# Gate and up projections of a feed-forward layer: two of eight weight chunks as seven block products, and a reciprocal cut in four

## The chip, the cores and the metric

The kernel runs on one core of a Trainium2 chip. The metric is the device time of one execution in microseconds, given as the median of several runs. The core has a matrix engine (TensorE, PE in the profile; its weight loads are listed apart as PEld), a vector engine (VectorE, DVE), a scalar engine (ScalarE, ACT), GpSimd (POOL) and a sync engine (SyncE, SP) that issues most of the transfers. Each engine works through its own instructions in the order in which they stand in its program.

## The reference, cut to what matters

One layer of a streaming encoder on 256 tokens of 2048 features, in float32. The first two thirds of the layer are four token mixers behind one wide projection; the last third is a feed-forward layer. What the change touches is the feed-forward layer and one expression of the gated linear attention:

```python
def gla_mixer(zg, w_a2, b_a, head_gain):            # gated linear attention
    ...
    log_a = jax.nn.log_sigmoid(w_lr @ w_a2 + b_a) / GLA_LOGIT_NORM
    ...
def reference(x, ...):
        ...
        h = rms_norm(x, norm_ffn_pre[l])
        ffn = (jax.nn.silu(h @ w_gate[l]) * (h @ w_up[l])) @ w_down[l]
        x = x + rms_norm(ffn, norm_ffn_post[l])
```

`w_gate` and `w_up` are 2048 x 5632, `w_down` is 5632 x 2048.

## The kernel before

Every large product is made of three: each float32 operand is split into a part `hi` that the matrix engine takes as it is and a rest `lo`, and hi·hi, hi·lo and lo·hi are added up in PSUM (lo·lo is left out).

Weights arrive in chunks of 256 rows by 512 columns (512 KB, `Stream.chunk`, L590 to L602): SP issues the transfer into one of four buffers `raw`; ACT casts `raw` to `hi` (L600); DVE subtracts to get `lo` (L601). Three pairs hi, lo exist at a time. A scheduler orders the instructions of each engine by its own cost model; the chunks' cast and subtraction have a raised priority, so that they run one or two chunks ahead of the products.

`gemm_tok` (L661 to L663) multiplies with the activations as the stationary operand (128 rows by 128 tokens) and the weights as the moving one (512 columns). A chunk has two row blocks of 128 and the tokens two halves of 128, so a chunk is 2 x 2 x 3 = 12 products of 512 columns. `gemm_feat` (L692, L693, L695) has it the other way round, the weights stationary and 256 tokens moving; it is used in the first third of the kernel.

The feed-forward part runs over 11 column groups `g` of 512 columns. For each, `gemm_tok` does 8 chunks of `w_gate` into two PSUM banks (one per token half) and 8 chunks of `w_up` into two others. When a gate column is done, ACT takes the sigmoid (L1044) and DVE forms the silu (L1045); when the up column is done, DVE multiplies (L1048), PE transposes the result block by block into a bank `tq` (L1053; eight small products per group) and ACT copies it to the buffer `aT` (L1054). After the eleven groups the down projection starts: ACT casts `aT` to `ah` (L1063), DVE makes `al` (L1064), and PE multiplies with the chunks of `w_down` (L1075 to L1077). All eight PSUM banks are in use: four `mm`, four `tq`, which the down projection's `wd` replaces.

In the gated linear attention, well ahead of this, one reciprocal over 128 x 512 numbers stands on DVE (L421) between the chunk work of a projection that runs at the same time.

## Time and profile before

| | us |
|---|---|
| median of 3 runs | 1647.31 (1645.69 to 1647.57) |
| the profiled execution | 1645.97 |
| its span, first to last instruction | 1644.2 |
| PE busy | 1630.3 (99%) |
| PEld busy | 1384.2 (84%) |
| DVE busy | 994.8 (61%) |
| ACT busy | 759.6 (46%) |
| POOL busy | 33.1 (2%) |
| granted clock of PE, mean | 0.998 of full |

Busy time of PE is counted from the start of a product to its modelled end, and products overlap; how fast products follow one another is therefore read from the difference of their starts in the timeline, not from the duration beside them. A weight load is a separate instruction that stands ahead of each product.

### The profile page before, as it was taken

How to read it: one execution, taken by the hardware profiler on the slowest of the kernel's cores; microseconds unless marked ns; L12 is line 12 of the kernel's file. 1: busy time of each engine (PE TensorE's matmuls, PEld its weight loads, DVE VectorE, ACT ScalarE, POOL GpSimd, SP SyncE). 2: the span in 40 equal slices, each digit the busy share in tenths (PEclk: the TensorE clock that was granted, in tenths of full speed). 3: DMA queues.
4: the chain of work that ended last, by engine and by line, in shares of the span. 5: the costliest groups of instructions: out<-in, count | busy, mean ns of one | idle time of the engine just before them, and what ended most of it. 6: DMA issues, size and time to landing. Idle time of an engine off the chain costs nothing.

```text
span 1644.2 us, 21813 instructions
## 1 busy us (share of the span) xinstructions
PE 1630.3 (99%) x8632; PEld 1384.2 (84%) x8632; DVE 994.8 (61%) x1176; ACT 759.6 (46%) x879; POOL 33.1 (2%) x46
## 2 busy tenths in 40 slices
PE   9999999999999999999999999999999999999997
PEld 9999988887789978888888888888888888888886
DVE  7568784669764477455655655444544555556555
ACT  6353443346554355444444644444444444445443
POOL 0000110000000001000000000000000000000000
PEclk9999999999999999999999999999999999999999
DMA  8554565345556545765555565555555555555563
GB/s 297 181 168 149 180 213 178 130 143 165 171 164 196 187 158 184 269 192 184 190 192 196 191 191 190 186 189 191 191 187 189 188 193 191 190 194 191 193 194 139
DMA packets 86118, 306.84 MB, mean 187 GB/s; under 512 B 9600, under 2 KB 12176, under 8 KB 85504
## 3 DMA queue, kind: packets, MB, share of 16 engines
q1 hardware_dynamic: 84352, 298.85, 55.6%
q0 software_dynamic: 1232, 5.95, 1.2%
q8 instruction: 67, 1.10, 0.3%
q10 hardware_dynamic: 432, 0.66, 0.2%
q14 instruction: 35, 0.29, 0.1%
HBM read 302.40 MB, written 3.01 MB: 186 GB/s over the span
## 4 chain that ended last, share of the span: by engine, by line
PE 97%; issue 1%; ACT 1%; DVE 1%; DMA 0%; POOL 0%; DVEq 0%; POOLq 0%; ACTq 0%
PE mm L662 22%; PE mm L663 21%; PE mm L661 21%; PE mm L692 5%; PE mm L693 4%; PE mm L695 4%; PE mm L1075 2%; PE mm L1077 2%; PE mm L1076 2%; PE wd L1077 2%; PE wd L1076 2%; PE wd L1075 2%; PE tq L1053 1%; PE mm L679 0%; PE ps L465 0%
## 5 line engine op out<-in xcount | busy, mean ns | idle before, releaser
L601 DVE TENSOR_TENSOR lo<-raw,hi 128x1024 fp32r<-128x1024 f32 (+1 forms) x554 | 676.6, 1222 | 550.9 <-ACT hi L600 548.7
L600 ACT CAST hi<-raw 128x1024 fp32r<-128x1024 f32 (+1 forms) x554 | 582.4, 1051 | 721.4 <-PE mm L663 510.1
L662 PE MATMUL mm<-lo,h_hi 128*128 128x512 f32 x704 | 274.9, 390 | 0.0
L663 PE MATMUL mm<-hi,h_lo 128*128 128x512 f32 x704 | 273.9, 390 | 0.1
L661 PE MATMUL mm<-hi,h_hi 128*128 128x512 f32 x704 | 250.6, 391 | 0.2 <-ACT h_hi L361 0.2
L662 PE MATMUL mm<-lo,hT_hi 128*128 128x512 f32 x608 | 238.8, 393 | 2.3 <-DVE lo L601 2.3
L663 PE MATMUL mm<-hi,hT_lo 128*128 128x512 f32 x608 | 237.5, 391 | 0.0
L661 PE MATMUL mm<-hi,hT_hi 128*128 128x512 f32 x608 | 219.5, 391 | 0.0
L692 PE MATMUL mm<-hT_hi,hi 128*128 128x256 f32 (+2 forms) x640 | 178.8, 284 | 0.3 <-ACT hi L600 0.3
L693 PE MATMUL mm<-hT_lo,hi 128*128 128x256 f32 (+2 forms) x640 | 177.1, 281 | 0.3 <-DVE hT_lo L362 0.3
L695 PE MATMUL mm<-hT_hi,lo 128*128 128x256 f32 x576 | 161.6, 282 | 0.0
L661 PEld LDWEIGHTS mm<-hi,h_hi 128*128 128x128 f32 x704 | 132.2, 188 | 27.8 <-ACT h_hi L361 0.9
L663 PEld LDWEIGHTS mm<-hi,h_lo 128*128 128x128 f32 x704 | 132.2, 188 | 27.6 <-DVE s L643 0.5
L662 PEld LDWEIGHTS mm<-lo,h_hi 128*128 128x128 f32 x704 | 132.2, 188 | 27.0
L662 PEld LDWEIGHTS mm<-lo,hT_hi 128*128 128x128 f32 x608 | 114.2, 188 | 27.2 <-DVE lo L601 2.7
L661 PEld LDWEIGHTS mm<-hi,hT_hi 128*128 128x128 f32 x608 | 114.1, 188 | 24.1
L663 PEld LDWEIGHTS mm<-hi,hT_lo 128*128 128x128 f32 x608 | 114.2, 188 | 23.6 <-issue 0.3
L692 PEld LDWEIGHTS mm<-hT_hi,hi 128*128 128x128 f32 (+2 forms) x640 | 119.8, 187 | 2.1 <-ACT hi L600 0.8
L693 PEld LDWEIGHTS mm<-hT_lo,hi 128*128 128x128 f32 (+2 forms) x640 | 120.1, 188 | 1.4 <-DVE hT_lo L362 0.5
L695 PEld LDWEIGHTS mm<-hT_hi,lo 128*128 128x128 f32 x576 | 108.7, 189 | 0.6
L1077 PE MATMUL mm<-hi,al 128*128 128x512 f32 x168 | 65.4, 389 | 0.0
L1076 PE MATMUL mm<-lo,ah 128*128 128x512 f32 x168 | 65.4, 389 | 0.0
(367 smaller groups left out, 1688.3 us busy)
## 6 DMA issues: line engine op xcount, KB each, us to landing
raw<-in_w_in_dram SPq DMA_DIRECT2D x224, 512.0 KB, 3.5
raw<-in_w_gate_dram SPq DMA_DIRECT2D x88, 512.0 KB, 3.5
raw<-in_w_up_dram SPq DMA_DIRECT2D x88, 512.0 KB, 3.5
raw<-in_w_down_dram SPq DMA_DIRECT2D x88, 512.0 KB, 3.5
raw<-in_w_branch_dram SPq DMA_DIRECT2D x32, 512.0 KB, 4.0
raw<-in_w_out_dram SPq DMA_DIRECT2D x32, 512.0 KB, 3.5
raw<-in_w_l_dram SPq DMA_DIRECT2D x8, 464.0 KB, 7.3
xs<-in_x_dram POOLq DMA_DIRECT2D x1, 2048.0 KB, 12.2
```

The costliest lines, as they stand in the source:

```text
L600: nc.scalar.copy(hi[:, :, :w], raw[:, :, :w])
L601: nc.vector.tensor_tensor(lo[:, :, :w], raw[:, :, :w], hi[:, :, :w].bitcast(F32), op=ALU.subtract)
L661: mm(banks[i_], ah[:, ts], hi[:, k, :], start=kt == 0, stop=False)
L662: mm(banks[i_], ah[:, ts], lo[:, k, :], start=False, stop=False)
L663: mm(banks[i_], al[:, ts], hi[:, k, :], start=False, stop=kt == nk - 1)
L692: mm(ps, hi[:, k, cs], hT_hi[:, kt, :], start=first, stop=False, skip_group_check=True)
L693: mm(ps, hi[:, k, cs], hT_lo[:, kt, :], start=False, stop=False, skip_group_check=True)
L695: mm(ps, lo[:, k, cs], hT_hi[:, kt, :], start=False, stop=last, skip_group_check=True)
L1053: T.transpose(ps[:, k, i * 128:(i + 1) * 128], sg[:, i, (2 * kp + k) * 128:(2 * kp + k + 1) * 128], ident)
L1075: mm(bk[j][i], ah[:, k, ts], hi[:, k, :], start=kt == 0, stop=False)
L1076: mm(bk[j][i], ah[:, k, ts], lo[:, k, :], start=False, stop=False)
L1077: mm(bk[j][i], al[:, k, ts], hi[:, k, :], start=False, stop=kt == 43)
```

## The change

In the groups g = 1 to 10, chunks 2 and 5 of each gate column and each up column (40 chunks in all) are no longer 12 products of 512 columns. The chunk is taken as a 2 x 2 matrix of blocks (128 rows by 256 columns each) and the tokens' part as 2 x 2 blocks of 128, and the product of the two is formed by the Winograd form of Strassen's scheme: 7 block products instead of 8, each of them three products (hi and lo) of 256 columns, so 21 products of 256 columns. Three of the seven use raw weight blocks and come first in the new buffers; four use sums of blocks. For that:

- DVE builds the sums of weight blocks in a buffer `t` (L1205 to L1207: 512, 256 and 256 columns), ACT casts seven blocks instead of four (in two pieces, 768 and 1024 columns), and DVE subtracts seven (L1212).
- The sums of activation blocks are built once, in group 0, on POOL (ten operations), ACT and DVE (`Seven.sums`).
- Partial results that belong to more than one output gather in two further banks `px` and `py`, which take the place of two of the four `tq` banks; at the end of each column `close` (L1234 to L1241) adds them up: ACT copies one block, DVE does three additions, and two more with the banks `mm`. The results lie in a buffer `w7`, and the sigmoid, the silu and the multiplication read them there.
- The down projection's buffers (`ah`, `al`, `fg`, `sqf`, the second gain) come from a pool `F2` that is opened after the pool `U` of the new buffers is closed, in the same memory. The transfer of the second gain moves behind the eleven groups.
- The reciprocal becomes four of 128 x 128.

Three places of the engines' programs show what moves. PE where the last up column ends and the down projection begins; before (L663 is the last up column, L1075 to L1077 the down projection, L1053 the transposes of the last group):

```order
L1075 MATMUL mm<-hi,ah 128x512 x2
L1076 MATMUL mm<-lo,ah 128x512
L1077 MATMUL mm<-hi,al 128x512
L1075 MATMUL mm<-hi,ah 128x512
L1076 MATMUL mm<-lo,ah 128x512
L1077 MATMUL mm<-hi,al 128x512
L1076 MATMUL mm<-lo,ah 128x512
L1077 MATMUL mm<-hi,al 128x512
L1075 MATMUL mm<-hi,ah 128x512
L1076 MATMUL mm<-lo,ah 128x512
L1077 MATMUL mm<-hi,al 128x512
L1053 MATMUL tq<-ident,sg 128x128 x8
```

and now (L663 to L665 the up column, L1084 the transposes, L1109 to L1111 the down projection):

```order
L665 MATMUL mm<-hi,h_lo 128x512
L663 MATMUL mm<-hi,h_hi 128x512
L664 MATMUL mm<-lo,h_hi 128x512
L665 MATMUL mm<-hi,h_lo 128x512
L1084 MATMUL tq<-ident,sg 128x128 x8
L1109 MATMUL mm<-hi,ah 128x512
L1110 MATMUL mm<-lo,ah 128x512
L1109 MATMUL mm<-hi,ah 128x512
L1110 MATMUL mm<-lo,ah 128x512
L1111 MATMUL mm<-hi,al 128x512
```

The transposes stood behind eleven entries of the down projection; now they stand ahead of its first product.

DVE around one column's end, before (L601 is a chunk's `lo`, L1045 the silu of a gate column, L1048 the multiplication after an up column):

```order
L1045 SCALAR_TENSOR_TENSOR sg<-mm,r_8015,sg 128x512
L601 TENSOR_TENSOR lo<-raw,hi 128x1024 x7
L1048 TENSOR_TENSOR sg<-sg,mm 128x512 x2
L601 TENSOR_TENSOR lo<-raw,hi 128x1024 x8
L1045 SCALAR_TENSOR_TENSOR sg<-mm,r_8015,sg 128x512
L601 TENSOR_TENSOR lo<-raw,hi 128x1024
L1045 SCALAR_TENSOR_TENSOR sg<-mm,r_8015,sg 128x512
L601 TENSOR_TENSOR lo<-raw,hi 128x1024 x7
L1048 TENSOR_TENSOR sg<-sg,mm 128x512 x2
```

and now, one column's end (L1205 to L1207 and L1212 the sums and rests of a chunk in seven blocks, L1235 to L1241 the closing sums, L1072 the silu; the number behind a name is a buffer's):

```order
L1235 TENSOR_TENSOR w_12059<-w_12059,px 128x256
L1236 TENSOR_TENSOR w_12059<-w_12059,py 128x256
L1237 TENSOR_TENSOR w_12059<-py,w_12059 128x2x256
L1205 TENSOR_TENSOR t<-raw 128x512
L604 TENSOR_TENSOR lo<-raw,hi 128x1024
L1206 TENSOR_TENSOR t<-t,raw 128x256
L1212 TENSOR_TENSOR lo_12184<-raw,hi_12183 128x768
L1241 TENSOR_TENSOR w_12059<-w_12059,mm 128x512 x2
L1207 TENSOR_TENSOR t<-t,raw 128x256
L604 TENSOR_TENSOR lo<-raw,hi 128x1024
L1072 SCALAR_TENSOR_TENSOR sg<-w_12059,r_8018,sg 128x512 x2
L604 TENSOR_TENSOR lo<-raw,hi 128x1024
```

Between two runs of `lo` there were two instructions; now the pieces of two seven-block chunks and the closing sums are mixed in.

DVE around the reciprocal, before (L421 is the reciprocal, L601 the `lo` of chunks, L422 to L426 what the attention does with the reciprocal):

```order
L421 RECIPROCAL h<-h 128x512
L601 TENSOR_TENSOR lo<-raw,hi 128x1024 x3
L422 TENSOR_TENSOR x<-x,h 128x512
L423 TENSOR_TENSOR s_3899<-x 128x512
L601 TENSOR_TENSOR lo<-raw,hi 128x1024
L424 TENSOR_SCALAR h<-s_3899 128x512
L426 SCALAR_TENSOR_TENSOR h<-h,s_3899 128x512 x2
```

and now (the same steps are L424 to L429, `lo` is L604):

```order
L424 RECIPROCAL h<-h 128x128 x4
L604 TENSOR_TENSOR lo<-raw,hi 128x1024 x3
L425 TENSOR_TENSOR x<-x,h 128x512
L426 TENSOR_TENSOR s_3899<-x 128x512
L427 TENSOR_SCALAR h<-s_3899 128x512
L429 SCALAR_TENSOR_TENSOR h<-h,s_3899 128x512
L604 TENSOR_TENSOR lo<-raw,hi 128x1024
```

The four pieces stand one behind the other, and the same three `lo` behind all of them; the next `lo` has moved behind two more steps of the attention.

The diff:

```diff
--- before.py
+++ after.py
@@ -418,7 +418,10 @@
     S.activation(x, x, AF.Exp, scale=-1.0)
 
     V.tensor_scalar(h, x, 2.0, None, op0=ALU.add)
-    V.reciprocal(h, h)
+    for j in range(2):
+        for p in range(2):
+
+            V.reciprocal(h[:, j, p * 128:(p + 1) * 128], h[:, j, p * 128:(p + 1) * 128])
     V.tensor_tensor(x, x, h, op=ALU.mult)
     V.tensor_tensor(s2, x, x, op=ALU.mult)
     V.tensor_scalar(h, s2, 1.0 / 17, None, op0=ALU.mult)
@@ -620,6 +623,7 @@
         e.dram = ctx.enter_context(tc.tile_pool(name="dr", bufs=1, space=bass.MemoryType.DRAM))
         mmp = ctx.enter_context(tc.tile_pool(name="mmp", bufs=1, space=PSUM))
         stream = Stream(e, ring)
+        e.ring = ring
 
         def bank():
             return mmp.tile([128, 512], F32, tag="mm", name="mm", bufs=4)
@@ -642,6 +646,25 @@
 
             V.tensor_scalar(ssum, ssum, 1.0 / n, eps, op0=ALU.mult, op1=ALU.add)
             G.tensor_tensor(ssum, ssum, e.mhalf.to_broadcast(list(ssum.shape)), op=ALU.pow)
+
+        def gemm_seven(w, lhs, banks, seven):
+
+            px, py = seven.banks()
+            for kc in range(8):
+                if kc in seven.kcs:
+                    seven.products(kc, lhs, seven.chunk(w(kc)), banks, px, py, kc == seven.kcs[0])
+                    continue
+                hi, lo = stream.chunk(w(kc))
+                for k in range(2):
+                    kt = 2 * kc + k
+                    ah, al = lhs(kt)
+                    for i in range(2):
+                        ts = slice(i * 128, (i + 1) * 128)
+                        mm(banks[i], ah[:, ts], hi[:, k, :], start=kt == 0, stop=False, skip_group_check=True)
+                        mm(banks[i], ah[:, ts], lo[:, k, :], start=False, stop=False, skip_group_check=True)
+                        mm(banks[i], al[:, ts], hi[:, k, :], start=False, stop=kt == 15, skip_group_check=True)
+            with tc.high_priority(offset=e.boost):
+                return seven.close(banks, px, py)
 
         def gemm_tok(w, lhs, nk, banks, runs={}, into={}):
 
@@ -1032,26 +1055,37 @@
         with ExitStack() as fctx:
             F = fctx.enter_context(tc.tile_pool(name="F", bufs=1))
             aT = F.tile([128, 44, 256], F32, name="aT")
-            gain = F.tile([128, 2048], F32, name="gain2")
-            nc.gpsimd.dma_start(gain, post_ffn.unsqueeze(0).to_broadcast([128, 2048]))
-            with tc.tile_pool(name="tq", bufs=1, space=PSUM) as tq:
+            lhs2 = lambda kt: (h2_hi[:, kt], h2_lo[:, kt])
+            with tc.tile_pool(name="U", bufs=1) as U, tc.tile_pool(name="tq", bufs=1, space=PSUM) as tq:
+                seven = Seven(e, U, tq, (2, 5))
                 for g in range(11):
                     bg, bu = [bank(), bank()], [bank(), bank()]
-                    lhs2 = lambda kt: (h2_hi[:, kt], h2_lo[:, kt])
                     sg = F.tile([128, 2, 512], F32, tag="sg", name="sg", bufs=2)
-                    gemm_tok(columns(w_gate, g), lhs2, 16, bg, {0: 3} if g == 0 else {})
+                    if g == 0:
+                        gemm_tok(columns(w_gate, g), lhs2, 16, bg, {0: 3})
+                        zg = bg
+                        seven.sums(h2_hi, h2_lo)
+                    else:
+                        zg = gemm_seven(columns(w_gate, g), lhs2, bg, seven)
                     for i in range(2):
-                        S.activation(sg[:, i], bg[i], AF.Sigmoid, scale=r2[:, i, 0:1])
-                        V.scalar_tensor_tensor(sg[:, i], bg[i], r2[:, i, 1:2], sg[:, i], op0=ALU.mult, op1=ALU.mult)
-                    gemm_tok(columns(w_up, g), lhs2, 16, bu)
+                        S.activation(sg[:, i], zg[i], AF.Sigmoid, scale=r2[:, i, 0:1])
+                        V.scalar_tensor_tensor(sg[:, i], zg[i], r2[:, i, 1:2], sg[:, i], op0=ALU.mult, op1=ALU.mult)
+                    if g == 0:
+                        gemm_tok(columns(w_up, g), lhs2, 16, bu)
+                        zu = bu
+                    else:
+                        zu = gemm_seven(columns(w_up, g), lhs2, bu, seven)
                     for i in range(2):
-                        V.tensor_tensor(sg[:, i], sg[:, i], bu[i], op=ALU.mult)
+                        V.tensor_tensor(sg[:, i], sg[:, i], zu[i], op=ALU.mult)
                     for kp in range(2):
-                        ps = tq.tile([128, 2, 256], F32, tag="tq", name="tq", bufs=4)
+                        ps = tq.tile([128, 2, 256], F32, tag="tq", name="tq", bufs=2)
                         for k in range(2):
                             for i in range(2):
                                 T.transpose(ps[:, k, i * 128:(i + 1) * 128], sg[:, i, (2 * kp + k) * 128:(2 * kp + k + 1) * 128], ident)
                         S.copy(aT[:, 4 * g + 2 * kp:4 * g + 2 * kp + 2], ps)
+            F = fctx.enter_context(tc.tile_pool(name="F2", bufs=1))
+            gain = F.tile([128, 2048], F32, name="gain2")
+            nc.gpsimd.dma_start(gain, post_ffn.unsqueeze(0).to_broadcast([128, 2048]))
             wd = fctx.enter_context(tc.tile_pool(name="wd", bufs=1, space=PSUM))
             fg = F.tile([128, 2, 2048], F32, name="fg")
             sq = F.tile([128, 512], F32, name="sqf", bufs=2)
@@ -1127,6 +1161,88 @@
                     (nc.sync, nc.scalar)[g % 2 * i].dma_start(outr[:, i, cs], fg[:, i, cs])
 
 
+class Seven:
+    def __init__(self, e, pool, psum, kcs):
+        self.e, self.pool, self.psum, self.kcs = e, pool, psum, kcs
+        n = len(kcs)
+        pad = lambda name, w: pool.tile([128, w], F32R, name=name)
+        self.s_hi, self.s_lo = (pad(n_, 4 * 128 * n).rearrange("p (c b t) -> p c b t", c=n, b=4) for n_ in ("s_hi", "s_lo"))
+
+    def sums(self, h_hi, h_lo):
+
+        e, nc = self.e, self.e.nc
+        G = nc.gpsimd
+        for c, kc in enumerate(self.kcs):
+            t = self.pool.tile([128, 4, 256], F32, tag="t", name="t", bufs=2)
+            h, s = t[:, 0:2], t[:, 2:4].rearrange("p x (b t) -> p (x b) t", t=128)
+            G.tensor_tensor(h, h_hi[:, 2 * kc:2 * kc + 2].bitcast(F32), h_lo[:, 2 * kc:2 * kc + 2].bitcast(F32), op=ALU.add)
+            a11, a21, a12, a22 = h[:, 0, 0:128], h[:, 0, 128:256], h[:, 1, 0:128], h[:, 1, 128:256]
+            G.tensor_tensor(s[:, 0], a21, a22, op=ALU.subtract)
+            G.tensor_tensor(s[:, 2], a11, a21, op=ALU.subtract)
+            G.tensor_tensor(s[:, 1], s[:, 0], a11, op=ALU.subtract)
+            G.tensor_tensor(s[:, 3], a12, s[:, 1], op=ALU.add)
+            nc.scalar.copy(self.s_hi[:, c], s)
+            nc.vector.tensor_tensor(self.s_lo[:, c], s, self.s_hi[:, c].bitcast(F32), op=ALU.subtract)
+
+    def banks(self):
+
+        return [self.psum.tile([128, 2, 256], F32, tag=n, name=n, bufs=1) for n in ("px", "py")]
+
+    def chunk(self, ap):
+
+        e, nc = self.e, self.e.nc
+        G = nc.vector
+        with e.tc.high_priority(offset=e.boost):
+            raw = e.ring.tile([128, 2, 512], F32, tag="raw", name="raw", bufs=e.nraw)
+            nc.sync.dma_start(raw, ap)
+            b = raw.rearrange("p k (c n) -> p (k c) n", c=2)
+            t = self.pool.tile([128, 4, 256], F32, tag="t", name="t", bufs=2)
+            G.tensor_tensor(t[:, 0:2], b[:, 1:3], b[:, 0:1].to_broadcast([128, 2, 256]), op=ALU.add)
+            G.tensor_tensor(t[:, 2], t[:, 0], b[:, 2], op=ALU.add)
+            G.tensor_tensor(t[:, 3], t[:, 2], b[:, 3], op=ALU.add)
+            hi, lo = (self.pool.tile([128, 1920], F32R, tag=n, name=n, bufs=2)[:, 48:1840].rearrange("p (b n) -> p b n", n=256)
+                      for n in ("hi7", "lo7"))
+            for x, o in ((b[:, 1:4], slice(0, 3)), (t, slice(3, 7))):
+                nc.scalar.copy(hi[:, o], x)
+                nc.vector.tensor_tensor(lo[:, o], x, hi[:, o].bitcast(F32), op=ALU.subtract)
+        return hi, lo
+
+    def products(self, kc, lhs, ch, banks, px, py, first):
+
+        mm = self.e.nc.tensor.matmul
+        hi, lo = ch
+        c = self.kcs.index(kc)
+        a = lambda k, i: tuple(x[:, i * 128:(i + 1) * 128] for x in lhs(2 * kc + k))
+        s = lambda b: (self.s_hi[:, c, b], self.s_lo[:, c, b])
+        for (ah, al), b, ps, st in ((a(0, 0), 0, px[:, 0], first), (a(1, 0), 2, banks[0][:, 256:512], False),
+                                    (s(3), 1, banks[0][:, 0:256], False), (s(0), 3, py[:, 1], first), (s(2), 4, py[:, 0], False),
+                                    (s(1), 5, px[:, 1], False), (a(1, 1), 6, banks[1][:, 256:512], False)):
+            mm(ps, ah, hi[:, b], start=st, stop=False, skip_group_check=True)
+            mm(ps, ah, lo[:, b], start=False, stop=False, skip_group_check=True)
+            mm(ps, al, hi[:, b], start=False, stop=kc == self.kcs[-1], skip_group_check=True)
+
+    def close(self, banks, px, py):
+
+        nc = self.e.nc
+        V = nc.vector
+        w = self.pool.tile([128, 5, 256], F32, tag="w7", name="w7", bufs=1)
+        nc.scalar.copy(w[:, 2], px[:, 0])
+        V.tensor_tensor(w[:, 0], w[:, 2], px[:, 1], op=ALU.add)
+        V.tensor_tensor(w[:, 4], w[:, 0], py[:, 0], op=ALU.add)
+        V.tensor_tensor(w[:, 1:4:2], py[:, 1:2].to_broadcast([128, 2, 256]), w[:, 0:5:4], op=ALU.subtract)
+        out = []
+        for i in range(2):
+            o = w[:, 1 + 2 * i:3 + 2 * i].rearrange("p b n -> p (b n)")
+            V.tensor_tensor(o, o, banks[i], op=ALU.add)
+            out.append(o)
+        return out
+
+
 class TagPool:
 
 
```

## Rows read from the trace of the kernel before

**Rows 1.** The page: engines' busy time, chain of waits, one DMA issue (landing us last).
```profile
PE 1630.3 (99%) x8632; PEld 1384.2 (84%) x8632; DVE 994.8 (61%) x1176; ACT 759.6 (46%) x879; POOL 33.1 (2%) x46
...
PE 97%; issue 1%; ACT 1%; DVE 1%; DMA 0%; POOL 0%; DVEq 0%; POOLq 0%; ACTq 0%
...
raw<-in_w_gate_dram SPq DMA_DIRECT2D x88, 512.0 KB, 3.5
```

**Rows 2.** The longest wait of PE: engine line waited for: us, times, longest.
```profile
PE mm L662 <- DVE lo L601: 2.3, 1, 2.3
```

**Rows 3.** Timeline of PE (start, us, instruction), gate and up products, 512 columns.
```profile
1001.01 0.40 PE L662 MATMUL mm<-lo,h_hi 128*128 128x512 f32 x1
...
1011.23 0.39 PE L662 MATMUL mm<-lo,h_hi 128*128 128x512 f32 x1
```

**Rows 4.** Timeline of PE where 256-column products stand, three places.
```profile
308.51 0.39 PE L663 MATMUL mm<-hi,oT 128*128 128x512 f32 x1
308.74 0.28 PE L692 MATMUL mm<-hT_hi,hi 128*128 128x256 f32 x1
...
309.56 0.28 PE L693 MATMUL mm<-hT_lo,hi 128*128 128x256 f32 x1
...
329.45 0.28 PE L692 MATMUL mm<-hT_hi,hi 128*128 128x256 f32 x1
...
332.85 0.28 PE L692 MATMUL mm<-hT_hi,hi 128*128 128x256 f32 x1
...
515.70 0.28 PE L692 MATMUL mm<-hT_hi,hi 128*128 128x256 f32 x1
...
516.88 0.28 PE L693 MATMUL mm<-hT_lo,hi 128*128 128x256 f32 x1
```

**Rows 5.** Busy time by window: PE, PEld, DVE, ACT, POOL, clock, DMA share, GB/s.
```profile
540.00:560.00 20.00, 20.00 (x173) 20.00 (x172) 8.79 (x8) 7.34 (x7) 0.00 (x0) 1.00 0.56 190
1000.00:1100.00 100.00, 100.00 (x453) 82.97 (x452) 49.65 (x45) 43.92 (x47) 0.00 (x0) 1.00 0.57 188
```

**Rows 6.** Groups of instructions by line: count, busy us, mean ns, idle before.
```profile
L601 DVE TENSOR_TENSOR lo<-raw,hi 128x1024 fp32r<-128x1024 f32 x546 | 667.7, 1223 | 549.7 <-ACT hi L600 547.5 <-issue 1.8
L600 ACT CAST hi<-raw 128x1024 fp32r<-128x1024 f32 x546 | 574.8, 1053 | 717.2 <-PE mm L663 510.1 <-PE mm L693 128.7 <-PE mm L1077 53.5
...
L1063 ACT CAST ah<-aT 128x512 fp32r<-128x512 f32 x44 | 27.5, 624 | 56.0 <-PE wd L1076 56.0
...
L1045 DVE SCALAR_TENSOR_TENSOR sg<-mm,r,sg 128x512 f32<-128x512 f32 x22 | 16.4, 747 | 5.4 <-ACT sg L1044 5.4
...
L1048 DVE TENSOR_TENSOR sg<-sg,mm 128x512 f32<-128x512 f32 x22 | 14.0, 679 | 0.0
...
L362 DVE SCALAR_TENSOR_TENSOR hT_lo<-acc,vec,hT_hi 128x256 fp32r<-128x256 f32 x16 | 6.7, 479 | 0.0
...
L458 ACT ACT_TABLE_LOAD x2 | 2.6, 1283 | 0.0
```

**Rows 7.** The sigmoid line L1044: durations, first and last start.
```profile
L1044 ACT ACTIVATE sg<-mm,r x22: 677/688/690, 928.3 to 1373.8; 128x512 f32<-128x512 f32 x22
```

**Rows 8.** Timeline around the end of the last up product, PE, then DVE.
```profile
1394.15 0.39 PE L663 MATMUL mm<-hi,h_lo 128*128 128x512 f32 x1
1394.37 0.61 PE L1075 MATMUL mm<-hi,ah 128*128 128x512 f32 x2
...
1397.10 1.04 PE L1053 MATMUL tq<-ident,sg 128*128 128x128 f32 x8
...
1394.08 1.28 DVE L1048 TENSOR_TENSOR sg<-sg,mm 128x512 f32<-128x512 f32 x2
```

**Rows 9.** Timeline around the reciprocal, DVE, then the PE row that waits.
```profile
372.17 3.34 DVE L421 RECIPROCAL h<-h 128x512 f32<-128x512 f32 x1
375.43 3.42 DVE L601 TENSOR_TENSOR lo<-raw,hi 128x1024 fp32r<-128x1024 f32 x3
...
376.64 0.50 PE L662 MATMUL mm<-lo,hT_hi 128*128 128x512 f32 x1 [2.29 <-DVE lo L601]
```

## The prediction

> **What bounds the kernel now.** I read the page first: PE is busy 99% of the span and the chain that ended last runs through PE for 97% [rows 1]. Next the waits of PE: the longest is one of 2.3 us for a `lo`, and nothing else is worth a microsecond once the kernel has started [rows 2]. So time is won only by fewer or quicker products, and is lost wherever another engine lets PE stand. Then the timeline of PE inside the gate and up columns: 45 products lie between 1001.01 and 1011.23, so one of 512 columns takes 0.2271 us [rows 3], and a chunk of 12 takes 2.725 us. A column group lasts (1373.8 - 928.3) / 10 = 44.55 us by the sigmoid's first and last start [rows 7]. In this stretch DVE is busy 49.65 of 100 us and ACT 43.92, PE's weight loads 82.97 [rows 5]. DVE and ACT have room, half of it at most.
>
> **The products of the seven-block chunks.** 40 chunks change from 12 x 512 columns to 21 x 256. What one of 256 costs is read where such products run now, and the trace shows two levels. From 308.74 to 309.56 seven steps, 0.117 us each; from 515.70 to 516.88 ten steps, 0.118; from 329.45 to 332.85 thirty steps, 0.1133 [rows 4]. The lower level is half of a 512-column step. At the upper level the weight loads are busy all of the time, 20.00 of 20 us [rows 5], so there the loads and not the moving columns seem to set the pace. The first two places are those where 256-column products follow directly on 512-column ones (308.51 is the last of these before the first place), and that is how a seven-block chunk stands between its neighbours; so I take 0.118. A chunk then takes 21 x 0.118 = 2.478 us, 0.247 less than 2.725, and 40 of them save **9.9 us**. At 0.1133 a chunk takes 2.379, and 40 save 13.8 us. The change would gain nothing at a step of 2.725 / 21 = 0.1298, which no row comes near.
>
> A rule of the Trainium skill speaks to this (page "TensorE: Matmul & The Clock Gate", section "Back-to-back issue gap"): an isolated product follows the last after N / 2.4 + 2.5 ns on a full clock, and in a stream of loads and products both set the distance. By its formula 256 columns take 109.2 ns and 512 take 215.8, which would save 2.590 - 2.293 = 0.297 us a chunk, 11.9 us in all. The rows stand above both figures, and the measurement decides; the second half of the rule agrees with the loads at 100%.
>
> **The work for DVE and ACT.** DVE's prices: 1.223 us for 1024 columns (L601) and 0.679 for 512 (L1048) [rows 6], that is 1.06 ns a column and 0.136 us fixed, by which 256 columns take 0.41 and 768 take 0.95 (the nearest row of 256, L362, has 0.479). A seven-block chunk costs DVE 0.68 + 0.41 + 0.41 for the sums and 0.95 + 1.22 for the rests, 3.67 us instead of 1.22. The closing sums of a column cost 0.41 + 0.41 + 3 x 0.68 = 2.86. A column group then has 12 x 1.223 + 4 x 3.67 + 2 x 2.86 + 2 x 0.747 + 2 x 0.68 = 37.9 us of DVE work in 44.55 - 4 x 0.247 = 43.56 us: 87% where there was half. ACT has per chunk 0.84 + 1.05 instead of 1.05 (between L1063's 0.624 for 512 columns and L600's 1.053 for 1024), and a small copy per column: about 24 us a group. Since both prepare chunks ahead, I walked one column through DVE's order: at a column's end the closing sums wait for PE's last product, and behind them stand a `t`, a `lo` and the pieces of the next column's first seven-block chunk. The `lo` of the second chunk of a column still comes about 3.4 us before PE needs it, the silu's products about 2.6 us before the transposes. DVE also waits for transfers in order now, since the sums read `raw` and not ACT's cast; a transfer lands 3.5 us after its issue [rows 1], and I find about 1 us of such waiting per column, within the 43.56 - 37.9 = 5.7 us that a group has free. I cost all of it at **nothing**; if the cover is gone it costs what rival C says. The sums of the activations run once, beside 16 chunks of group 0 that do not need them, and delay the first sigmoid by at most 2 us, when its PSUM bank is not asked for until 22 us later: nothing. The later transfer of the second gain is needed half a down projection later: nothing.
>
> **The border to the down projection.** Before, the first down product starts 0.22 us after the last up product [rows 8], and the transposes stand eleven entries later; DVE multiplies in that time (1394.08 to 1395.36). Now the transposes stand first, behind the closing sums (DVE 2 x 0.68), the multiplication (2 x 0.64, of rows 8), and `ah` waits for the last multiplication too, since its buffer overlies `w7`. The first closing sum needs only the bank of the first token half, which is done three products earlier, so it lies beside them. From that product's start I count 0.2 us to its end, 0.68 for the second closing sum, 1.28 for the multiplications (the transposes of the first half start in between), 0.1 for a semaphore and 0.62 for the cast to `ah` (L1063) [rows 6]: the first down product at about +2.9, and 0.3 us more until the first `al`. Of the 3.2 us the eight transposes fill 0.8, which were on the path before as well. That leaves **2.4 us** of new idle time, once; from 1.5 (the engines overlap better) to 4 (a `lo` of the next chunk gets between).
>
> **The reciprocal.** It holds DVE from 372.17 to 375.43, and the `lo` behind it is the one that PE waits 2.29 us for [rows 9]. The four pieces stand back to back, and the same `lo` behind all of them; so nothing gets in between, and the wait stays. By the fixed part of 0.136 us less an overlap of 0.08, four pieces take 3.43 instead of 3.26: **+0.2 us** (0 to 0.4).
>
> **The linear attention behind it.** The scheduler has moved work by about one chunk: the fourth `lo` stands behind two more steps on DVE, some 1.1 us. PE needs it three chunks after the one it waited for, at 376.64 + 3 x 2.725 = 384.8; DVE was done with it at about 375.43 + 3.42 + 2 x 0.68 + 1.2 = 381.4 [rows 9, 6]. So this is hidden. On ACT two loads of function tables (1.28 us each [rows 6]) with their exponentials stand ahead of two casts. My walk gives a wait between 0 and 0.3 us; I take **+0.3** (-0.5 to +4, if both loads fall on the path with a cast behind them).
>
> **Sum.** -9.9 + 2.4 + 0.2 + 0.3 = -7.0 us. On the profiled execution of 1645.97 that is 1639.0. The median of the runs is 1.34 us above that execution, so against the median I say **1640**.
>
> **Rivals.**
> A, the forecast: 1640, its own range 1638 to 1643.5 (by the border's and the attention's bounds). 52%.
> B, the 256-column products run at 0.1133. For it: this level lasts for long stretches, and the loads are then just under full. Against: both places that follow on 512-column products show the other. -13.8 + 2.9 = -10.9, so 1636.4. 22%.
> C, DVE comes too late in every column. In its queue an instruction that waits (for PE's last product, for a transfer, for ACT's cast) holds all behind it, the `lo` of the next chunks too. As soon as these waits sum to more than 5.7 us a group, DVE sets the pace; at 6.65 the ten groups take as long as before. My walk has about 2 us a group, but the order was made by a cost model and not by the chip, and PE's order has plain chunks broken up there to wait for a `lo`, which shows that the model sees DVE close. With 7 us of waits a group takes 44.9: +3.5 us in ten groups and +2.9 elsewhere, 1653.7. 13%.
> That queues of DVE and ACT are strictly first in, first out is also what the Trainium skill states (same page, section "Architectural detail: the array is 16× 32×32, not 1× 128×128"); by it a late closing sum cannot be passed by a ready `lo`, which is C's mechanism, and the 2.29 us behind the reciprocal are a case of it.
> D, the gain comes but the one-off terms are at their upper ends: border 4, reciprocal 0.4, attention 4. -9.9 + 8.4 = -1.5, 1645.8, about no change. Against it: PE's waits in the attention are small now, and table loads there already lie beside products. 13%.
> The reciprocal in pieces doing nothing is part of A.
>
> **How the numbers follow.** A difference under 0.2%, 3.3 us, can't be told from no change. A and B lie below 1644, and of D a small part (3%): faster 0.77. The rest of D and a little of C: same 0.12. C and the end of D: slower 0.11. The range takes A and B with B's lower bound (border 1.5, attention -0.5: 1635) and D's bound up to 1648; C lies outside it.
>
> **What would show it.** In the changed profile: 256-column starts in the seven-block chunks 0.118 apart (B: 0.113); groups 43.6 us apart by the sigmoid; DVE near 87% in these windows, and no waits of PE for `lo`, `t` or `w7` inside the groups (C: one per column, of 0.2 us and more); one idle stretch of about 2.4 us before the first transposes and the first down product; the wait behind the reciprocal still there at about 2.4 us; no wait over 0.5 us in the attention. The forecast is wrong if PE stands inside the groups, or if 256-column steps come out over 0.125.

## The result: 1662.6 us, slower by 1%

The changed kernel took 1662.61 us in the median of 4 runs (1661.16 to 1663.18), the kernel before 1646.61 (4 runs). The ratio is 1.0096 with a 95% interval of 1.0084 to 1.0109. I had said 1640, in a range of 1635 to 1648. The profiled execution has a span of 1660.7 us against 1644.2: 16.5 us more.

The page of the kernel after, engines and the chain that ended last; they answer to [rows 1]:

```profile
PE 1628.5 (98%) x8992; PEld 1395.5 (84%) x8992; DVE 1126.7 (68%) x1441; ACT 788.1 (47%) x941; POOL 42.1 (3%) x56
...
PE 75%; DVE 9%; DMA 9%; issue 5%; ACT 2%; POOL 0%; DVEq 0%; POOLq 0%; ACTq 0%; SPq 0%
```

PE has even less busy time than before (1628.5 instead of 1630.3 us), though the span is longer: the time went into standing still. The chain runs through PE for only 75% now, and DVE and transfers (DMA) have 9% each, where they had 1% and 0%. Next, the three longest waits of PE (line and what it waited for: us in total, times, longest):

```profile
PE mm L664 <- DVE lo L604: 10.2, 8, 2.1
PE tq L1084 <- DVE sg L1079: 8.1, 14, 1.5
PE mm L685 <- DVE lo L604: 2.3, 1, 2.3
```

The last stood before as well [rows 2]. The first two are new: PE waits for the `lo` of plain chunks and for the products that it is to transpose, both made by DVE. Their waits make 16.7 us in the groups (1.65 of the 18.3 stand at the border to the down projection), less than the 22.7 that the groups lost (12.8 later, see below, with 9.9 saved in the products): a wait is counted from the modelled end of the product ahead of it, which lies some 0.16 us behind the point where the next could start (0.39 us long, 0.227 apart), and the shortest waits are not listed. And DVE in the same stretch, from the second column group to the last gate column:

```profile
DVE t L1205 <- DMA raw<-in_w_up_dram: 59.8, 18, 5.3
DVE t L1205 <- DMA raw<-in_w_gate_dram: 34.9, 18, 3.9
```

DVE stood at the first sum of a seven-block chunk (L1205) 36 times, 2.63 us each time and 94.7 us in all, until the chunk's transfer had landed. One such place, DVE and then SP, which issues the transfer:

```profile
1095.12 1.23 DVE L1212 TENSOR_TENSOR lo<-t,hi 128x1024 fp32r<-128x1024 f32 x1
1096.27 1.22 DVE L604 TENSOR_TENSOR lo<-raw,hi 128x1024 fp32r<-128x1024 f32 x1
1101.96 0.69 DVE L1205 TENSOR_TENSOR t<-raw 128x512 f32<-128x512 f32 x1 [4.47 <-DMA raw<-in_w_up_dram]
1102.57 1.22 DVE L604 TENSOR_TENSOR lo<-raw,hi 128x1024 fp32r<-128x1024 f32 x1
...
1094.04 1.46 SPq L596 DMA_DIRECT2D raw<-in_w_up_dram  x2
1097.51 0.33 SPq L1202 DMA_DIRECT2D raw<-in_w_up_dram  x1
```

The `lo` at 1096.27 ends at 1097.49 and with it the last use of a raw buffer; SP issues the transfer into that buffer at 1097.51; the sums that need it are the very next instruction on DVE, which stands still for 4.47 us with two more `lo` and a whole chunk's rests behind it. Two transfers of plain chunks of the up column stand ahead (1094.04), so this is its chunk 2. A column group then takes 46.2 us by the silu's first and last start, instead of 44.5 (the 44.55 of [rows 7] has the distance of the two halves still in it):

```profile
L1072 DVE SCALAR_TENSOR_TENSOR sg<-w,r,sg x20: 742/746/753, 977.6 to 1393.9; 128x512 f32<-128x512 f32 x20
```

That is (1393.9 - 977.6 - 0.7) / 9, where 0.7 is taken off for the distance of the two halves of the last one.

**The 16.5 us, place by place.** The transposes just ahead of the feed-forward part start at 901.53 and started at 901.54, so nothing before it changed the time. The last up product starts at 1406.92 instead of 1394.15 [rows 8]: +12.8 us. The first down product follows 3.22 us later instead of 0.22, of which the transposes (0.79 us, which stood later before) are no loss: +2.2. From there to the end it takes 250.6 us, before 249.8 with those transposes in it: +1.5. Sum 16.5. The border, PE:

```profile
1406.92 0.39 PE L665 MATMUL mm<-hi,h_lo 128*128 128x512 f32 x1
1408.79 0.44 PE L1084 MATMUL tq<-ident,sg 128*128 128x128 f32 x2 [1.49 <-DVE sg L1079]
...
1410.14 0.77 PE L1109 MATMUL mm<-hi,ah 128*128 128x512 f32 x1
...
1411.13 0.63 PE L1109 MATMUL mm<-hi,ah 128*128 128x512 f32 x1
1411.56 0.63 PE L1110 MATMUL mm<-lo,ah 128*128 128x512 f32 x1
...
1413.81 0.39 PE L1109 MATMUL mm<-hi,ah 128*128 128x512 f32 x1
1414.04 0.39 PE L1110 MATMUL mm<-lo,ah 128*128 128x512 f32 x1
```

The last 1.5 us are a clock: from 1410.14 to 1413.81 the products follow one another in 0.43 us (the first step in 0.56) instead of 0.227. The granted clock of two windows there (the third to last number of a row is its share of full speed):

```profile
1410.20:1413.80 3.60, 3.60 (x10) 2.87 (x10) 2.09 (x5) 1.85 (x4) 0.32 (x1) 0.55 0.75 239
1413.80:1420.00 6.20, 6.20 (x29) 5.11 (x28) 1.23 (x1) 1.58 (x2) 0.00 (x0) 1.00 0.55 200
```

It is at about half there (the lower of its two levels, 1.2 of 2.4 GHz) and full again afterwards; ahead of it PE had waited 1.49 us for the transposes' input and then had eight small products with a wait of 0.16 us among them.

What came as forecast is the price of the products. Sixteen of a seven-block chunk (first and last):

```profile
1022.21 0.28 PE L1225 MATMUL mm<-hi,h_hi 128*128 128x256 f32 x1
...
1023.97 0.28 PE L1227 MATMUL mm<-hi,h_lo 128*128 128x256 f32 x1
```

15 steps in 1.76 us, 0.117 each: the upper of the two levels of [rows 4]. Over the groups the median step from one such product to the next is 0.118.

### The profile page after: what moved, and what is told of

The parts are those of the page before. It is cut to its first block, busy times and chain, and to the rows that moved or that the text cites. A ratio compares the mean times of both kernels' runs of the same rounds, so it can differ in the third digit from the quotient of the medians.

```text
span 1660.7 us, 22833 instructions
## 1 busy us (share of the span) xinstructions
PE 1628.5 (98%) x8992; PEld 1395.5 (84%) x8992; DVE 1126.7 (68%) x1441; ACT 788.1 (47%) x941; POOL 42.1 (3%) x56
## 4 chain that ended last, share of the span: by engine, by line
PE 75%; DVE 9%; DMA 9%; issue 5%; ACT 2%; POOL 0%; DVEq 0%; POOLq 0%; ACTq 0%; SPq 0%
PE mm L685 13%; PE mm L686 13%; PE mm L684 13%; DMA raw<-in_w_up_dram 5%; DVE lo L604 5%; PE mm L715 4%; PE mm L716 4%; PE mm L718 4%; DMA raw<-in_w_gate_dram 4%; PE mm L1109 2%; PE mm L1110 2%; PE mm L1111 2%; PE wd L1110 2%; PE wd L1109 2%; PE wd L1111 2%
## 5 line engine op out<-in xcount | busy, mean ns | idle before, releaser
L604 DVE TENSOR_TENSOR lo<-raw,hi 128x1024 fp32r<-128x1024 f32 (+1 forms) x514 | 626.5, 1222 | 340.2 <-ACT hi L603 338.0
L603 ACT CAST hi<-raw 128x1024 fp32r<-128x1024 f32 (+1 forms) x514 | 537.7, 1049 | 517.7 <-PE mm L686 276.9
L664 PE MATMUL mm<-lo,h_hi 128*128 128x512 f32 x480 | 188.1, 392 | 10.3 <-DVE lo L604 10.2
L665 PE MATMUL mm<-hi,h_lo 128*128 128x512 f32 x480 | 187.2, 390 | 0.0
L663 PE MATMUL mm<-hi,h_hi 128*128 128x512 f32 x480 | 183.6, 390 | 0.0
L664 PEld LDWEIGHTS mm<-lo,h_hi 128*128 128x128 f32 x480 | 90.1, 188 | 28.8 <-DVE lo L604 12.1
L665 PEld LDWEIGHTS mm<-hi,h_lo 128*128 128x128 f32 x480 | 90.2, 188 | 18.2
L663 PEld LDWEIGHTS mm<-hi,h_hi 128*128 128x128 f32 x480 | 90.1, 188 | 17.3
L1211 ACT CAST hi<-raw 128x768 fp32r<-128x768 f32 x40 | 33.5, 836 | 135.5 <-DMA raw<-in_w_gate_dram 69.2
L1205 DVE TENSOR_TENSOR t<-raw 128x512 f32<-128x512 f32 x40 | 27.7, 693 | 98.6 <-DMA raw<-in_w_up_dram 61.6
```

What stands on the lines that cost most here:

```text
L603: nc.scalar.copy(hi[:, :, :w], raw[:, :, :w])
L604: nc.vector.tensor_tensor(lo[:, :, :w], raw[:, :, :w], hi[:, :, :w].bitcast(F32), op=ALU.subtract)
L663: mm(banks[i], ah[:, ts], hi[:, k, :], start=kt == 0, stop=False, skip_group_check=True)
L664: mm(banks[i], ah[:, ts], lo[:, k, :], start=False, stop=False, skip_group_check=True)
L665: mm(banks[i], al[:, ts], hi[:, k, :], start=False, stop=kt == 15, skip_group_check=True)
```

## The experiments

Theory 1: DVE's order has the sums of a seven-block chunk too close behind the instruction that frees the chunk's raw buffer. By the order, with the durations of [rows 6], DVE has 1.9 us of work between the two (0 to 3.6), a transfer takes 4.5 us to land, and 4.5 - 1.9 = 2.6 is the wait that the profile shows. The four seven-block chunks of a group bear it out one by one: with 0, 1.2, 2.6 and 3.6 us of work in between, DVE waits 4.5, 3.1, 2.1 and 0.8 us (means of nine). Since DVE is in order, the `lo` behind it are late for PE. Theory 2: DVE has too much work, wherever its waits are. Theory 3: the transfers themselves have become slow (4.5 us instead of the 3.5 of [rows 1]). All ratios below are to runs of the kernel before on the same chip, with 95% intervals.

**1. A buffer of their own for the raw weights of the seven-block chunks.**

```diff
-            raw = e.ring.tile([128, 2, 512], F32, tag="raw", name="raw", bufs=e.nraw)
+            raw = self.pool.tile([128, 2, 512], F32, tag="raw7", name="raw7", bufs=1)
```

> The raw weights of the seven-block chunks get a buffer of their own, so their transfers no longer wait for one of the four shared buffers to come free. Theory 1 (DVE, in order, stands waiting for these transfers: 94.7 us in 36 chunks, because the shared buffer is freed only by the lo that stands just ahead of the sums): the waits for transfers fall below 20 us, a column group takes 43.6 instead of 46.2 us, the time falls by 20 to 26 us to 1637 to 1643. Theory 2 (DVE's added work and its waits for PE at each column's end are too much by themselves, whatever the buffers): the waits move to another line and the time stays above 1655. Theory 3 (the transfers themselves are slower, 4.4 instead of 3.5 us to landing, since the memory is crowded): about half of the waits stay, some 1650.

1641.37 us, ratio 0.9968 (0.9957 to 0.9978): 21 us faster than the changed kernel, 5.3 faster than the one before by this ratio (6.0 between the medians). The waits of DVE:

```profile
DVE lo L604 <- ACT hi L603: 25.1, 26, 3.5
DVE t L1205 <- DMA raw<-in_w_gate_dram: 22.5, 18, 2.5
DVE t L1205 <- DMA raw<-in_w_up_dram: 19.6, 18, 2.6
DVE lo L1212 <- ACT hi L1211: 9.5, 14, 1.4
```

The waits for transfers fell from 94.7 to 42.1 us, not below 20 as I had written, but by about half, as theory 3 had it; its time, some 1650, did not come. PE waits for nothing in the groups any more, and a group takes 43.5 us by the starts of the transposes (1000.1 to 1348.0 in eight groups; the silu's starts give 43.2, since the last comes earlier in its group than the first). DVE does the same work as in the changed kernel, so theory 2 falls. The transfers still take 4.4 us (median), so slow transfers alone do not make the loss; they are a part of each wait all the same. The order now has 2.9 us of work between freeing and sums. The last up product starts at 1385.24, 8.9 us earlier than before, and the border costs 2.2: -6.7, and the span is 6.6 shorter.

**2. One seven-block chunk in a column instead of two** (`Seven(e, U, tq, (2,))`).

> Only chunk 2 of each column goes by seven products, chunk 5 is as before; the shared buffers stay. Theory 1: one wait of some 2.6 us per column stays, but a group has 31.6 us of DVE work and 5.2 of waiting in 44.1 us, so PE sets the pace again: 20 chunks save 4.9 us, the border to the down projection costs about 3, 1644.5. Theory 2 (work): the same work fits as well, 1644 to 1646. Both would be wrong if it is slower than 1650.

1646.49 us, ratio 0.9996 (0.9987 to 1.0006), just above both ranges, which lie so close that this run can't tell the theories apart. DVE waits only 14.1 us for transfers, 0.8 each, and PE for nothing in the groups, which take 44.1 us as worked out. The profiled span is 1644.8, 0.6 more than before: from the transposes ahead of the feed-forward part (903.1) to the last up product (1392.44) it takes 3.3 us less, the border costs 2.2, and this execution came to the feed-forward part 1.6 us later. That is a clock as well. Behind the wait of 2.3 us at the reciprocal [rows 9] PE's clock is at the lower level here, and was full in the kernel before; this run, then the kernel before:

```profile
377.00:380.40 3.40, 3.40 (x10) 2.61 (x9) 3.33 (x5) 0.00 (x0) 0.00 (x0) 0.51 0.74 233
377.00:380.40 3.40, 3.40 (x16) 2.80 (x15) 3.21 (x5) 1.06 (x1) 0.00 (x0) 1.00 0.73 227
```

So the spans of two profiled executions can differ by some 1.5 us at such a place. A part of the gain is there, too small to show.

**3. The sums on POOL instead of DVE** (`G = nc.gpsimd`).

> The sums of weight blocks are made on POOL instead of DVE, so DVE has 6 us less work in a group and no sum in its queue that waits for a transfer. Theory 1: the rest of the raw blocks on DVE still stands behind ACT's cast, which waits for the same late transfer, so a good part of the waiting stays under ACT's name: 1645 to 1655. Theory 2 (work alone): 30.5 us of work in 43.6, all of the loss is gone, about 1640. POOL too slow for four sums in 5 us would show as waits for POOL and a time above 1655.

1698.83 us, ratio 1.0316 (1.0301 to 1.0332): outside the ranges of both theories, and above the 1655 that I had set for a POOL that is too slow. DVE has less work, and the kernel is 36 us slower than with the sums on DVE. DVE's waits, and then its groups and POOL's (busy us, mean ns behind the count):

```profile
DVE lo L1212 <- ACT hi L1211: 132.0, 57, 6.2
...
L604 DVE TENSOR_TENSOR lo<-raw,hi 128x1024 fp32r<-128x1024 f32 x101 | 130.9, 1316 | 0.0
L1212 DVE TENSOR_TENSOR lo<-raw,hi 128x768 fp32r<-128x768 f32 x33 | 44.6, 1351 | 100.1 <-ACT hi L1211 100.1
...
L1072 DVE SCALAR_TENSOR_TENSOR sg<-w,r,sg 128x512 f32<-128x512 f32 x18 | 17.1, 957 | 0.0
...
L1207 POOL TENSOR_TENSOR t<-t,raw 128x256 f32<-128x256 f32 x40 | 55.8, 1394 | 3.1
L1206 POOL TENSOR_TENSOR t<-t,raw 128x256 f32<-128x256 f32 x40 | 53.5, 1337 | 3.1
L1205 POOL TENSOR_TENSOR t<-raw 128x512 f32<-128x512 f32 x40 | 51.9, 1297 | 327.0 <-DMA raw<-in_w_up_dram 173.7 <-DMA raw<-in_w_gate_dram 138.2 <-DVE lo L604 15.2
```

POOL takes 1.30 + 1.34 + 1.39 = 4.0 us for a chunk's sums and frees the raw buffer that much later; DVE's wait only changes its name to ACT's cast and grows from 94.7 to 132.0 us in the same window, where ACT in turn waits 155.7 us for transfers and 78.1 for POOL's sums. It speaks against theory 2 once more: DVE is occupied for 33.4 us a group instead of 35.2, and that did not help: a group takes 49.8 us. Two things are mixed in here, the later freeing and DVE's own instructions, which became longer beside POOL's (below), so it is no measure of either.

**4. The reciprocal in four pieces, alone, in the kernel before.**

> The kernel before with nothing changed but the reciprocal in four pieces. Theory: the pieces stand back to back, so the wait behind them stays at 2.3 us and the time is the same within 0.1% (1646.6, between -1 and +1 us). The rival (the pieces let a lo through): 2.3 us faster.

1647.44 us, ratio 1.0002 (0.9993 to 1.0011). DVE and the row of PE that waits, to lay beside [rows 9]:

```profile
372.15 3.38 DVE L423 RECIPROCAL h<-h 128x128 f32<-128x128 f32 x4
375.44 3.42 DVE L603 TENSOR_TENSOR lo<-raw,hi 128x1024 fp32r<-128x1024 f32 x3
...
PE mm L664 <- DVE lo L603: 2.3, 1, 2.3
```

Four pieces hold DVE for 3.29 us instead of 3.26, and the wait behind them is the same. This part of the change does nothing.

**5. The border: the cast `ah` in memory of its own**, on top of experiment 1.

```diff
-            F = fctx.enter_context(tc.tile_pool(name="F2", bufs=1))
+            Fh, F = F, fctx.enter_context(tc.tile_pool(name="F2", bufs=1))
-                    ah = F.tile([128, 2, 256], F32R, tag="ah", name="ah", bufs=3)
+                    ah = Fh.tile([128, 2, 256], F32R, tag="ah", name="ah", bufs=3)
```

> As the first experiment (own buffer for the raw weights of seven-block chunks), and the down projection's cast ah lies in memory that no other buffer shares, so that it no longer waits for the last multiplication, and the scheduler puts four down products ahead of the last transposes. Theory: of the 2.9 us by which the border was later, the wait of 1.5 us and the cast go, 1.5 to 2.5 us faster than the first experiment: 1639 to 1640. The rival (the border's wait only moves to al, or to the transposes a little later): no faster than the first experiment.

1641.49 us, ratio 0.9973 (0.9964 to 0.9982): no faster than experiment 1. The first down product now starts at once, and the wait has moved:

```profile
PE wd L1109 <- ACT aT L1085: 0.8, 1, 0.8
PE tq L1084 <- DVE sg L1079: 0.7, 2, 0.6
```

0.7 us for the transposes' input and 0.8 for a PSUM bank `wd`, which takes the place of a `tq` that ACT has yet to read: 1.5 us instead of the 1.6 in experiment 1. The rival was right in the main: the wait moved, though to the transposes and to a bank, not to `al`.

**6. Four raw buffers as in the changed kernel, but three shared and one kept for the seven-block chunks** (experiment 1 with 3 for `e.nraw`).

> The same number of raw buffers as the changed kernel, four, but three are shared and one is kept for the seven-block chunks. It tells whose buffer it is from how many there are. Theory 1 as I put it (the seven-block chunk's transfer waits for the lo that stands just ahead of its sums, because it shares the ring): a column group takes under 44.5 us, though other stages may be slower with three. The rival (one buffer more was all that helped): a group takes 46 us or more, since the plain chunks now come late instead.

1648.89 us, ratio 1.0015 (1.0005 to 1.0026). It is the stage that counts here:

```profile
L1072 DVE SCALAR_TENSOR_TENSOR sg<-w,r,sg x20: 741/743/747, 984.0 to 1375.4; 128x512 f32<-128x512 f32 x20
```

A group takes (1375.4 - 984.0 - 0.7) / 9 = 43.4 us (43.7 by the starts of the transposes), against 46.2 with four shared ones; what three buffers cost, they cost ahead of it (the first start is 6.4 us later than in the changed kernel). So it is not how many buffers there are, but when the one that is waited for comes free: the one own buffer is freed by the rests of the raw blocks of the seven-block chunk before (L1212), and DVE has 3.0 us of work from there to the next sums instead of 1.9.

**7. Three seven-block chunks in a column** (1, 3 and 5; experiment 1 otherwise).

> As the first experiment, with three of eight chunks in seven blocks (1, 3 and 5). PE's products alone would give 43.2 - 0.5 = 42.7 us a group, 5 us less in all than the first experiment. DVE's work is then some 36.5 + 2 x 2.3 = 41.1 us a group, 96%. Theory: with so little room every wait in DVE's queue (the closing sums for PE, the sums for transfers, 4 to 8 us a group) delays PE: a group takes 44 to 48 us and the time is 1648 to 1685. The rival (DVE's waits shrink by themselves when it has no room, as it never runs ahead): about 42.8, 1637.

1701.86 us, ratio 1.0338 (1.0321 to 1.0355), worse than the range of the theory. A group takes (1432.5 - 983.4 - 0.7) / 9 = 49.8 us; PE waits 42 us in all, for the casts and rests of the seven-block chunks and for the transposes' input, and its granted clock is below full for parts of the stretch (0.95 from 1100 to 1200). The direction is that of the theory, DVE without room; of the size, I had no right sum, since SP now waits 130.9 us (from 975 to 1360) for sums to free the one own buffer, which I had not counted.

**8. Two buffers of their own** (experiment 1 with `bufs=2`).

> As the first experiment, with two buffers of their own for the raw weights of the seven-block chunks instead of one. In the first experiment DVE still waited 42 us for these transfers in 36 chunks, but PE waited for nothing inside the groups. Theory: DVE's waits for transfers fall below 20 us, and the time is that of the first experiment within 2 us (1639 to 1643), since PE was not held up. The rival (what DVE still waits costs something that the list of PE's waits does not show): 3 us or more faster.

1645.76 us, ratio 0.9993 (0.9984 to 1.0002): 4 us slower than experiment 1, against both expectations. With a second buffer the scheduler puts the sums further ahead, so that DVE has 3.0 us of work between freeing and sums, hardly more than with one (2.9); a transfer takes 4.7 us here:

```profile
DVE t L1205 <- DMA raw<-in_w_up_dram: 32.9, 18, 3.4
DVE t L1205 <- DMA raw<-in_w_gate_dram: 24.5, 17, 2.4
...
PE tq L1084 <- DVE sg L1079: 3.8, 6, 1.5
```

57.4 us of waits where one buffer had 42.1, and PE waits six times at the transposes. A buffer more did not give distance, because the order spent it.

**9. Two seven-block chunks in gate columns, three in up columns** (one own buffer).

> As the first experiment (one own buffer), gate columns with two chunks in seven blocks (1, 5), up columns with three (1, 3, 5). PE's products alone save 10 x 0.247 = 2.5 us more; DVE has some 38.8 us of work in 43 us a group, 90%. If the room that DVE needs beside its work is the 4 to 5 us a group that it waits for transfers, ACT and PE, this is where it becomes late: theory 1645 to 1665, with waits of PE in the up columns. If three chunks were only too much together, 1639.

1643.32 us, ratio 0.9978 (0.9969 to 0.9988): faster than before, not faster than experiment 1, and between the theory's 1645 and the rival's 1639. PE's waits for the transposes' input grew to 4.2 us from 1.6, and 1.0 for a `lo` came in. DVE is busy 85% of the time from 1000 to 1348, in experiment 1 it is 82%. With experiment 7 this says that the room for DVE ends about here; what sets the end was not tested further.

**10. Only the order: the sums behind the `lo` of the plain chunk ahead.** The four shared buffers of the changed kernel stay; a copy of two columns makes the sums wait for that `lo`.

```diff
+            nc.vector.tensor_copy(t[:, 0, 0:2], prev[:, 1, 510:512].bitcast(F32))
             G.tensor_tensor(t[:, 0:2], b[:, 1:3], b[:, 0:1].to_broadcast([128, 2, 256]), op=ALU.add)
```

> The changed kernel with its four shared buffers, and only the order on DVE altered: a copy of two columns from the rest lo of the plain chunk ahead into the sums' buffer makes the sums of a seven-block chunk wait for that lo, so the scheduler puts them behind it. Between the instruction that frees the chunk's raw buffer and its sums now lie 8.5 us of DVE work by the order (before: 1.9 us, between 0 and 3.6), more than the 4.4 us that a transfer takes. Theory 1 (it is the place of the sums, not the number of buffers): DVE's waits at the sums fall from 95 us to under 15, a group takes 43 to 44 us, the time is 1638 to 1644. The rival (DVE waits as long in another place, since the transfer's buffer is freed by DVE in any order): above 1655.

1641.87 us, ratio 0.9968 (0.9958 to 0.9978), with the change's own buffers and one instruction more per chunk. DVE:

```profile
DVE lo L1213 <- ACT hi L1212: 56.8, 33, 3.9
DVE lo L604 <- ACT hi L603: 4.8, 12, 0.8
```

No wait for a transfer is left at the sums, though a transfer takes as long as in the changed kernel (4.5 us, median). The rests wait for ACT's cast now, which costs PE 0.8 us in all of the groups, and a group takes 43.7 us. This settles it: the buffers are those of the changed kernel, DVE has an instruction more, only the order is another (the scheduler moved neighbours of the sums along with them), and 21 us are gone.

**11. Both: later sums and two own buffers.**

> The later sums of the run above and two buffers of their own for the raw weights of the seven-block chunks: 14 us of DVE work between the freeing of a buffer and the sums. Theory 1: no waits for transfers at the sums at all, PE never waits in the groups, 1638 to 1641, at best 2 us under the first experiment. The rival (the sums now come so late that ACT's cast and the rests are late for PE): waits of PE for the rests of the seven-block chunks, 1645 or more.

1639.85 us, ratio 0.9957 (0.9944 to 0.9971): the fastest here, 7.2 us under the kernel before and 23 under the changed one. PE busy, and then weight loads, DVE and ACT, by window:

```profile
1000.00:1100.00 100.00, 100.00 (x553) 87.11 (x552) 80.10 (x112) 53.28 (x62) 0.00 (x0) 1.00 0.57 193
1100.00:1200.00 100.00, 100.00 (x535) 86.52 (x534) 84.56 (x121) 53.04 (x60) 0.00 (x0) 1.00 0.59 195
1200.00:1300.00 100.00, 100.00 (x547) 86.95 (x547) 81.59 (x113) 52.49 (x60) 0.00 (x0) 1.00 0.57 194
```

The profile shows no idle time of PE in the groups, with DVE at 80 to 85%.

## Why the prediction was wrong

The step that failed is the sentence "I find about 1 us of such waiting per column", of DVE's waits for transfers. It was 94.7 / 18 = 5.3 us. With 10.5 us a group instead of 2 DVE set the pace: rival C, to which I had given 13% and a price of 1653.7. The price was too low because I had put in 7 us of waits.

The room that I had set against these waits, 5.7 us, was mis-sized as well, in the other direction. My 37.9 us of DVE work adds up the durations of instructions, and these overlap by some 0.06 us each. DVE's occupied time is the fourth of the times in this row:

```profile
975.00:1392.00 417.00, 400.18 (x2143) 343.95 (x2142) 318.05 (x418) 198.08 (x237) 0.00 (x0) 1.00 0.55 182
```

That is 318.05 / 417 x 46.2 = 35.2 us a group, which leaves 8.3 us in the 43.5 that PE needs. 35.2 + 10.5 + 0.3 = 46.0 is the group as measured, to 0.2 us, and only the 0.3 are waits for ACT, by which PE had held DVE back before (547.5 us in [rows 6]). DVE is paced by its own work and the transfers, and PE follows it.

Most of what was needed to see it was at hand: four raw buffers, each freed by DVE itself, 3.5 us to landing [rows 1], and an order in which the sums of an up column's chunk 2 stand directly behind the `lo` that frees their buffer. What was not at hand is that a transfer would take 4.5 us to land. With 3.5 the same order would give some 6.4 us of waits a group, and DVE 41.9 us, less than PE needs: by this estimate from these rows, the order and the slower landing made DVE late together. Experiment 10 shows that another order is enough to undo it; no run takes away the slower landing alone.

I took DVE's place in time from what PE needs, as if DVE reached the sums late; but the order has them as early as a buffer can be free in the scheduler's model, and DVE waits there with all that PE needs next behind it. Before the change this could not happen, since `lo` waits for ACT's cast, which waits for a buffer that PE frees: DVE was held back by PE and never came upon a transfer.

The other steps:
- 256-column products at 0.118: measured 0.117 (the formula that I quoted from the Trainium skill's page "TensorE: Matmul & The Clock Gate", section "Back-to-back issue gap", gives 0.109; the trace decides). The loads at 100%, from which I argued that they set this pace, do not tell the two levels apart: from 329.45 to 332.85, at 0.1133, they are busy 3.40 of 3.40 us as well. Where DVE is in time, the groups take 8.9 us less (experiment 1) and 10.5 less (experiment 11, from the transposes ahead of the feed-forward part); I had said 9.9.
- DVE's prices held: its instructions from 975 to 1392 add up to 345 us, 38.2 a group where I had 37.9. What they do not say is the time that DVE is taken (above). It was not the work.
- The border: 2.4 forecast, 2.2 measured, and 1.5 for the clock behind it, which I did not have. In experiment 1 the same wait of 1.49 us stands there without the slow clock, in experiments 6, 9 and 10 it is there again. The 0.1 us for a semaphore in my sum stands in no row; where DVE waits for ACT's result it starts 0.03 us behind its end.
- The reciprocal, +0.2: below what shows (3.29 instead of 3.26 us on DVE). The linear attention, +0.3: 0.0.
- My sum of -7.0 us is what experiments 1 and 11 give (-6.6 and -6.0 of span, -6.0 and -7.2 between the medians), kernels in which DVE is in time; experiment 11 came to the feed-forward part 2.2 us later, with the clock at 0.57 from 377.0 to 380.4. Rivals B (0.1133) and D (one-off terms) are out.

What stays open: why the clock fell at the border in the profiled executions of the changed kernel and of experiments 6, 9 and 10 and not in those of 1, 2, 8 and 11, with much the same wait (1.48 to 1.58 us); what makes transfers land later in the changed kernels, beyond their lying over one another (below); and how much of experiment 3 is POOL's pace and how much the longer instructions of DVE.

## What to carry to other kernels

When an engine with room takes over work that reads a transfer directly, look up in the order what stands between the instruction that frees the buffer and the one that reads it anew, and set its time against the landing; the share of busy time does not show it. Take the work from occupied time and not from a sum of durations. In an in-order queue an instruction that the scheduler's model places too early can do as much harm as one that comes late, and another buffer helps only if the order leaves the distance (experiments 8 and 10). Work out what ends the wait of each engine before: an engine that was paced by the bottleneck loses that when its input changes.

## What the runs showed of the hardware

- A wait of 1.5 us on PE can be followed by a stretch at half the clock (granted 0.55 from 1410.2 to 1413.8 in the changed kernel, 0.53, 0.53 and 0.51 at the same place in experiments 6, 9 and 10), and need not: behind the same wait in experiments 1, 2, 8 and 11 the clock stayed full. So too behind the wait of 2.3 us at the reciprocal: 0.51 in experiment 2, 1.00 in the kernel before.
- DVE's instructions grow longer beside POOL's. In experiment 3 POOL is busy 32% of the time from 975 to 1392. The `lo` of 1024 columns took 1217 ns where no POOL instruction ran beside it (63 of them; 1219 in the changed kernel) and 1575 where one did for over 90% of its time (24). The silu of 512 took 746 without and 1221 with; the subtraction of 768 columns, always beside POOL, took 1351 (954 in the changed kernel). The additions L1241, which read a PSUM bank, did not grow: 676 ns (681). POOL's additions took 1.30 us for 512 columns and 1.34 to 1.39 for 256; what they take without DVE beside them, no run shows.
- A transfer of 512 KB took 3.5 us to land in the kernel before, where they are issued 2 to 3 us apart, and 4.4 to 4.7 for the seven-block chunks of the changed kernel and of experiments 1 and 8. In the changed kernel the median is 3.5 us for transfers with on average half of another or less under way beside them, 4.4 with one, 4.6 with one and a half.
